# A delta rule's set-up in another order: the products for the inverse first, the other chunk products beside the substitution, their masks on GpSimd

## The chip, the core and the metric

The kernel runs on one core of a Trainium2 chip. The metric is the device time of one execution in microseconds (us), as the median of several runs of the same program. A core has five engines that run their own instruction streams and wait for one another by semaphores: TensorE (PE in the profile; its weight loads are PEld), VectorE (DVE), ScalarE (ACT), GpSimd (POOL) and SyncE (SP), which starts DMA transfers. Matrix products go to PSUM, a memory of eight banks, from which VectorE and ScalarE read them; everything else lies in SBUF, with 128 partitions.

## The reference

Two layers of a decoder trunk on one sequence of 512 tokens with 1024 channels, all in float32. Each layer has a feed-forward block, three token mixers on the same normalised input (an RWKV-7 delta rule, latent attention, an HGRN2 recurrence), whose outputs are gated and merged, and a second feed-forward block. The change is in the first mixer. It has 8 heads of 64 channels, and its state is updated token by token:

```python
def rwkv7_scan(r, w, k, v, kk, a):
    ...
    def step(state, inp):
        r_t, w_t, k_t, v_t, kk_t, a_t = inp
        sa = jnp.einsum('bhvk,bhk->bhv', state, -kk_t)
        state = (state * w_t[:, :, None, :]
                 + sa[..., None] * (kk_t * a_t)[:, :, None, :]
                 + v_t[..., None] * k_t[:, :, None, :])
        return state, jnp.einsum('bhvk,bhk->bhv', state, r_t)
```

## The kernel before

**Chunks instead of tokens.** The kernel cuts the 512 tokens into 8 chunks of 64 and handles a chunk at a time. Within a chunk it needs triangular matrices of products between tokens: for each head and chunk the left factors are two kinds of key (beta, which is `kk*a`, and the key `k`, together the tensor `BK`), and the right factors two kinds of query (alpha, the removal key, and rho, the receptance; together `AR`). Of these four products per chunk and head, beta·alpha gives a unit triangular matrix that has to be inverted; key·alpha multiplies the values later; and the two with rho go into the output. Each product is masked to its triangle.

**`rwkv_invert`** (from L463) makes these products, masks them and inverts. For each of four pairs of heads, 16 matmuls (L481) compute all four kinds at once: 128 weight columns by 128 moving columns, from 64 rows. They go into two PSUM banks at a time (the names `b` in the trace; three banks, 2 to 4, take turns under the use "a"). VectorE multiplies each full bank of 128x512 by the triangular mask on its way to SBUF (L484, 16 per layer). ScalarE then cuts the 32x32 diagonal blocks of beta·alpha out into one tile (L487, 16 copies per layer), VectorE transposes that tile (L489), and 31 steps of a forward substitution follow on VectorE, each a multiplication (L500) and a subtraction (L501). In step j the multiplication reads column j of the blocks, `a[:, j + 1:, j]`, whose elements lie 32 elements apart; `ti` is the inverse as it grows. GpSimd fills `ti` with zeros and a diagonal of ones beforehand (L492, L493). Two transposes (L504, L505) bring the result into the two forms that the next step needs. That next step (L522 and L525, small matmuls of 32x32) puts the 64x64 inverse together from its 32x32 blocks, and its first matmul needs the second transpose.

**`rwkv_scan`** follows: key·alpha times the values (L565) and then a loop over the eight chunks (L581 to L615).

**What else runs there.** TensorE has other work that doesn't depend on this chain: 41 column blocks of projections for the other two mixers and for the gates, in three matmuls per 128x128 weight (L251, L252, L253; 24 per block), called fillers here. Each weight is split first, into a rounded part on ScalarE (L208) and a rest on VectorE (L209). `pump` pulls blocks of them into the program at places named by a table, and a scheduler then sets a fixed order for each engine from the program's order, the data's dependencies and the buffers. In both layers fillers stand between the products and L522. In layer 0 the rotary key of the attention mixer runs there as well (VectorE L901 to L904 and L930, ScalarE L906, one matmul L932, ScalarE's copy L934), and it uses the same three PSUM banks.

Of the kernel before, what the change touches and what calls it, by code (L numbers as in the profile page):

```python
# [15 lines left out]
ALU = mybir.AluOpType  # L16
# [4 lines left out]
P = 128  # L21
# [3 lines left out]
NT = T // P  # L25
# [4 lines left out]
CH = 64  # L30
NC = T // CH
# [275 lines left out]
class Rwkv:  # L307
# [155 lines left out]
    def rwkv_invert(self):  # L463


        nc = self.nc
        S = self.S
        GM = S["GM"] = [self.slot(i, (P, 2, NC, P)) for i in (0, 1, 6, 7)]
        ad = self.m4((P, 4, 2, NT, 32))
        mask = self.c("tri").unsqueeze(1).broadcast_to([P, 4, P])  # L470
        for p in range(4):
            self.pump("A4", p)

            for i in range(2):
                ps = [self.psum("a", (P, 4, P)) for _ in range(2)]
                for c in range(4):
                    cc = 4 * i + c
                    for e in range(2):
                        q = slice(64 * e, 64 * e + 64)
                        bk = S["BK"][p // 2][q, p % 2].rearrange("p t z x -> p (t z x)")  # L480
                        nc.tensor.matmul(ps[e][:, c, :], bk[:, P * cc:P * cc + P], S["AR"][p // 2][q, p % 2, :, cc * CH:(cc + 1) * CH],  # L481
                                         start=True, stop=True)
                for e in range(2):
                    nc.vector.tensor_mul(GM[p][:, e, 4 * i:4 * i + 4, :], ps[e], mask)  # L484
            for b in range(4):
                q = slice(32 * b, 32 * b + 32)
                nc.scalar.copy(ad[q, p], GM[p][q, :, b // 2::2, 32 * (b % 2):32 * (b % 2) + 32])  # L487
        ac = [self.m4((P, 32, 32)) for _ in range(2)]
        nc.vector.transpose(out=ac[0], in_=ad.rearrange("p a e t x -> p x (a e t)"))  # L489
        a, tmp = ac  # L490
        ti = self.m4((P, 32, 32))
        nc.gpsimd.memset(ti, 0.0)  # L492
        nc.gpsimd.memset(ti.rearrange("p s t -> p (s t)")[:, ::33], 1.0)  # L493
        for j in range(31):
            if j % 4 == 0:
                self.pump("A9", j // 4)
            n, m = j + 1, 31 - j
            acol = a[:, j + 1:, j].unsqueeze(1).broadcast_to([P, n, m])
            trow = ti[:, :n, j].unsqueeze(2).broadcast_to([P, n, m])
            nc.vector.tensor_mul(tmp[:, :n, :m], acol, trow)  # L500
            nc.vector.tensor_sub(ti[:, :n, j + 1:], ti[:, :n, j + 1:], tmp[:, :n, :m])  # L501

        td, tu = self.m4((P, 32, 32)), self.m4((P, 32, 32))
        nc.vector.transpose(out=td.rearrange("p n t -> p t n"), in_=ti.rearrange("p s t -> p t s"))  # L504
        nc.vector.transpose(out=tu.rearrange("p n s -> p s n"), in_=ti)  # L505
        S["tt"] = [self.slot(2, (P, 16, P)), self.slot(3, (P, 16, P))]
        for i in range(2):
            tt = S["tt"][i]
            nc.gpsimd.memset(tt, 0.0)
            for b in range(4):  # L510
                q = slice(32 * b, 32 * b + 32)
                nc.scalar.copy(tt[q, :, q], td[q, 16 * i:16 * i + 16, :])

            self.pump("A5", i)
            n21, x = self.psum("a", (P, 16, 32)), self.t2(shape=(P, 16, 32))
            for half in range(2):
                for n in range(16):
                    h, t = 4 * i + n // 4, n % 4
                    for u in range(2):
                        up, dn = slice(64 * u, 64 * u + 32), slice(64 * u + 32, 64 * u + 64)  # L520
                        if half == 0:
                            nc.tensor.matmul(n21[dn, n, :], GM[h // 2][up, h % 2, 2 * t + u, 32:64], tu[up, 16 * i + n, :],  # L522
                                             start=True, stop=True, tile_position=(64 * u, 64 * u + 32))
                        else:
                            nc.tensor.matmul(n21[up, n, :], x[dn, n, :], tt[dn, n, dn], start=True, stop=True,  # L525
                                             tile_position=(64 * u + 32, 64 * u))
                for u in range(2):
                    up, dn = slice(64 * u, 64 * u + 32), slice(64 * u + 32, 64 * u + 64)
                    if half == 0:
                        nc.scalar.copy(x[dn], n21[dn])  # L530
                    else:
                        nc.scalar.activation(tt[up, :, dn], n21[up], AF.Copy, scale=-1.0)

        for p in range(4):
            self.pump("A6", p)
            bk = S["BK"][p // 2][:, p % 2].rearrange("p t z x -> p (t z x)")
            tmp = [self.t2() for _ in range(2)]
            for i in range(2):
                dl = self.DL[:, p, 4 * i:4 * i + 4].unsqueeze(2).broadcast_to([P, 4, P])
                nc.vector.tensor_mul(tmp[i].rearrange("p (c x) -> p c x", x=P), bk[:, 512 * i:512 * i + 512].rearrange("p (c x) -> p c x", x=P), dl)  # L540
            for i in range(2):
                ps = self.psum("a", (P, 4, P))
                for c in range(4):
                    self.transpose(ps[:, c, :], tmp[i][:, c * P:(c + 1) * P])
                nc.scalar.copy(bk[:, 512 * i:512 * i + 512].rearrange("p (c x) -> p c x", x=P), ps)

    def rwkv_scan(self, l):


        nc = self.nc  # L550
        S = self.S
        GM, vn = S["GM"], S["vn"]
        U = [slice(0, 64), slice(64, 128)]
        al = lambda p: S["AR"][p // 2][:, p % 2, 0]
        rho = lambda p: S["AR"][p // 2][:, p % 2, 1]
        bk = lambda p, c: S["BK"][p // 2][:, p % 2].rearrange("p t (u z) x -> p (t u) (z x)", u=2)[:, c]
        gv = [self.m4((P, 2, 2, NT, CH)) for _ in range(2)]
        for p in range(4):
            self.pump("A7", p)
            ps = self.psum("a", (P, 2, NT, CH))  # L560
            for e in range(2):
                h = 2 * p + e
                for t in range(NT):
                    for u in range(2):
                        nc.tensor.matmul(ps[U[u], e, t, :], GM[p][U[1 - u], e, 2 * t + u, 0:64], vn[U[1 - u], t, 64 * h:64 * h + 64], start=True, stop=True)  # L565
            nc.scalar.copy(gv[p // 2][:, p % 2], ps)
        for c in range(NC):
            self.pump("A8", c)
            t, u = c // 2, c % 2
            ck = slice(c * CH, (c + 1) * CH)  # L570

            zv = self.t2(shape=(P, 4, 2, CH))
# [3 lines left out]
            else:  # L576
                r = self.t2(shape=(P, 4, 2, CH))
                ps = [self.psum("a", (P, 4, CH)) for _ in range(2)]
# [7 lines left out]
            z = self.psum("z", (P, 4, 2, CH))  # L586
            for p in range(4):
                for e in range(2):
                    h = 2 * p + e
                    nc.tensor.matmul(z[U[u], p, e, :], S["tt"][h // 4][U[u], (h % 4) * 4 + t, U[u]], rhs(p, e), start=True, stop=True)  # L590
            nc.scalar.activation(zv[U[u]], z[U[u]], AF.Copy, scale=-1.0)
            y = self.psum("y", (P, 4, CH))
# [13 lines left out]

            for p in range(4):
                for e in range(2):
                    nc.tensor.matmul(y[U[e], p, :], zv[:, p, e, :], GM[p][:, e, c, 64:], start=p == 0, stop=c == 0 and p == 3)
            if c:  # L610
                for p in range(4):
                    for e in range(2):
# [796 lines left out]
```

## Time and profile before

| | us |
|---|---|
| median of 3 runs | 2726.13 |
| lowest and highest | 2724.97, 2731.2 |
| the profiled execution | 2736.01 |
| its span in the trace | 2734.2 |
| TensorE busy | 2683.8 (98%) |
| VectorE busy | 1779.8 (65%) |
| ScalarE busy | 1347.4 (49%) |
| GpSimd busy | 58.5 (2%) |

The mean clock that TensorE was granted over this execution was 0.989 of full speed. In rows of the timeline the columns are start, duration, engine, line, operation, output and inputs (partitions x elements), and in brackets the idle time before it and what ended that. A float32 matmul has two records in the trace. "Fillers" are L251 to L253 there.

### The profile page before, as it was taken

The numbers are of one execution on the slowest core, as the hardware profiler recorded it, in microseconds if no ns is written. First come the engines' busy times: TensorE is split into PE (matmuls) and PEld (weight loads), VectorE is DVE, ScalarE is ACT, GpSimd is POOL, SyncE is SP. The second block draws the span as 40 slices with busy tenths as digits, with TensorE's granted clock in tenths as the row PEclk, the third lists the DMA queues.
The fourth block names the chain that finished last, engine by engine and source line by source line (L and its number), as shares of the span: only waits on it lengthen the run. The fifth ranks groups of instructions, "written<-read, shape, count | busy, mean of one in ns | idle before, by whom it ended". The sixth has DMA issues, their size and how long they took to land. (4 is left out here: it accounts for less than half of the span.)

```text
span 2734.2 us, 42594 instructions
## 1 busy us (share of the span) xinstructions
PE 2683.8 (98%) x17669; PEld 2331.5 (85%) x17669; DVE 1779.8 (65%) x2507; ACT 1347.4 (49%) x2133; POOL 58.5 (2%) x121
## 2 busy tenths in 40 slices
PE   8999999989999999999999999999899999999999
PEld 7999887777787789998889998877677878899987
DVE  6786447763866667875467864477558676678843
ACT  4444346245657644444334443464465685444532
POOL 0000010000000000000000000100000000100000
PEclk9999999899999999999999999999999999999999
DMA  4333332324422451233313233323253225423332
GB/s 142 108 109 123 124 117 91 102 74 155 158 82 67 158 189 62 96 127 116 126 40 116 93 125 126 112 90 108 82 194 111 94 69 180 146 87 99 107 118 77
DMA packets 223518, 307.72 MB, mean 113 GB/s; under 512 B 11856, under 2 KB 181052, under 8 KB 221788
## 3 DMA queue, kind: packets, MB, share of 16 engines
q1 hardware_dynamic: 223324, 304.99, 33.2%
q8 instruction: 139, 2.28, 0.3%
q14 instruction: 55, 0.45, 0.0%
HBM read 269.84 MB, written 35.13 MB: 112 GB/s over the span
## 5 line engine op out<-in xcount | busy, mean ns | idle before, releaser
L253 PE MATMUL b<-xhi,wl 128*128 128x256 f32 (+1 forms) x2176 | 734.9, 338 | 0.0
L251 PE MATMUL b<-xhi,wh 128*128 128x256 f32 (+1 forms) x2176 | 734.9, 338 | 0.0
L252 PE MATMUL b<-xlo,wh 128*128 128x256 f32 (+1 forms) x2176 | 734.2, 337 | 0.0
L208 ACT CAST wh<-ws 128x1024 fp32r<-128x1024 f32 (+5 forms) x448 | 393.1, 889 | 649.7 <-PE b L252 273.5
L209 DVE TENSOR_TENSOR wl<-ws,wh 128x1024 fp32r<-128x1024 f32 (+5 forms) x448 | 453.1, 1022 | 258.9 <-ACT wh L208 255.6
L251 PEld LDWEIGHTS b<-xhi,wh 128*128 128x128 f32 x2176 | 415.3, 191 | 45.4 <-issue 4.4
L252 PEld LDWEIGHTS b<-xlo,wh 128*128 128x128 f32 x2176 | 415.3, 191 | 41.5 <-issue 3.2
L253 PEld LDWEIGHTS b<-xhi,wl 128*128 128x128 f32 x2176 | 415.2, 191 | 41.2 <-issue 1.9
L251 PE MATMUL b<-s,wh 128*128 128x256 f32 (+1 forms) x1120 | 344.4, 307 | 1.3 <-DVE s L996 1.3
L252 PE MATMUL b<-s,wh 128*128 128x256 f32 (+1 forms) x1120 | 344.1, 307 | 0.0
L253 PE MATMUL b<-s,wl 128*128 128x256 f32 (+1 forms) x1120 | 344.1, 307 | 0.0
L208 ACT CAST wh<-m 128x1024 fp32r<-128x1024 f32 x144 | 151.2, 1050 | 231.0 <-PE b L252 100.8
L251 PE MATMUL b<-wh,t 128*128 128x512 f32 x576 | 224.2, 389 | 0.0
L252 PE MATMUL b<-wl,t 128*128 128x512 f32 x576 | 224.1, 389 | 0.0
L253 PE MATMUL b<-wh,t 128*128 128x512 f32 x576 | 224.1, 389 | 0.0
L251 PEld LDWEIGHTS b<-s,wh 128*128 128x128 f32 x1120 | 213.9, 191 | 11.9 <-DVE s L996 2.2
L253 PEld LDWEIGHTS b<-s,wl 128*128 128x128 f32 x1120 | 213.9, 191 | 10.1
L252 PEld LDWEIGHTS b<-s,wh 128*128 128x128 f32 x1120 | 213.9, 191 | 9.8
L209 DVE TENSOR_TENSOR wl<-m,wh 128x1024 fp32r<-128x1024 f32 x144 | 174.0, 1224 | 33.3 <-ACT wh L208 33.3
L209 DVE TENSOR_TENSOR t<-s,t 128x512 fp32r<-128x512 f32 x80 | 55.0, 691 | 158.6 <-PE b L252 154.2
L251 PEld LDWEIGHTS b<-wh,t 128*128 128x128 f32 x576 | 108.1, 188 | 23.1 <-ACT t L1194 0.6
L253 PEld LDWEIGHTS b<-wh,t 128*128 128x128 f32 x576 | 108.1, 188 | 22.4
(328 smaller groups left out, 4002.2 us busy)
## 6 DMA issues: line engine op xcount, KB each, us to landing
ws<-in_w_in_dram SPq DMA_DIRECT2D x58, 1024.0 KB
ws<-in_ffn_w_up_dram SPq DMA_DIRECT2D x44, 1024.0 KB
ws<-in_ffn_w_down_dram SPq DMA_DIRECT2D x44, 1024.0 KB
ws<-in_ffn_w_gate_dram SPq DMA_DIRECT2D x43, 1024.0 KB
gd<-f SPq DMA_DIRECT2D x48, 256.0 KB
t<-gd SPq DMA_DIRECT2D x48, 256.0 KB
s<-cd SPq DMA_DIRECT2D x8, 1024.0 KB
ws<-in_w_o_dram SPq DMA_DIRECT2D x8, 1024.0 KB
```

Source lines behind the costliest of these rows:

```text
L208: self.nc.scalar.copy(hi, src)
L209: self.nc.vector.tensor_sub(lo, src, hi.bitcast(F32))
L251: nc.tensor.matmul(out, whi, xhi, start=start, stop=False, **kw)
L252: nc.tensor.matmul(out, whi, xlo, start=False, stop=False, **kw)
L253: nc.tensor.matmul(out, wlo, xhi, start=False, stop=stop, **kw)
```

## The change

Products and masks are split by kind, and reordered:

- Each product is now of one kind: 64 weight columns by 64 moving columns (L479 of the changed kernel, function `product`), 256 per layer, four times as many as of L481, each a quarter of its size. Results for even and odd chunks go to different halves of a bank.
- The 64 beta·alpha products come first. VectorE masks them (L495, 4 per layer), ScalarE cuts out the diagonal blocks (L498, 16 copies as before), and VectorE transposes (L500).
- That transpose writes its output in another arrangement, so the substitution reads its column contiguously: `a[:, j, j + 1:]` (L528; the subtraction is L529).
- The other 192 products come behind this in the program. ScalarE copies each full bank to SBUF (L508, 12 per layer), and GpSimd multiplies it by the mask in place (L509, 12 per layer, 128x512, both operands in SBUF).
- The readers of the products index the new tiles. `pump("A4", ...)` has zeros in its table before and after.

The transposes behind the substitution are L532 and L533 now, the combining matmuls L550 and L553, the memsets on GpSimd L503, L504 and L537, the rotary key's steps L930 to L933, L959, L935, L961 and L963.

```diff
-        GM = S["GM"] = [self.slot(i, (P, 2, NC, P)) for i in (0, 1, 6, 7)]
+        GA, GR = S["GA"], S["GR"] = [[self.slot(i) for i in x] for x in ((0, 1), (6, 7))]
...
+        def product(out, p, e, c, z, i):
+            bk = S["BK"][p // 2][U[e], p % 2].rearrange("p t z x -> p (t z) x")
+            nc.tensor.matmul(out[U[z]], bk[:, 2 * c + z, :], S["AR"][p // 2][U[e], p % 2, i, c * CH:(c + 1) * CH], start=True, stop=True)
+        def alphas(i, y):
+            ps = [self.psum("a", (P, 2, NT, CH)) for _ in range(2)]
+            for k in range(2):
+                for c in range(NC):
                     for e in range(2):
-                        nc.tensor.matmul(ps[e][:, c, :], bk[:, P * cc:P * cc + P], S["AR"][p // 2][q, p % 2, :, cc * CH:(cc + 1) * CH],
-                                         start=True, stop=True)
-                for e in range(2):
-                    nc.vector.tensor_mul(GM[p][:, e, 4 * i:4 * i + 4, :], ps[e], mask)
-            for b in range(4):
-                nc.scalar.copy(ad[q, p], GM[p][q, :, b // 2::2, 32 * (b % 2):32 * (b % 2) + 32])
+                        product(ps[e][:, k, c // 2, :], 2 * i + k, e, c, (c + y) % 2, 0)
+            return [x.rearrange("p k t x -> p (k t) x") for x in ps]
+        for i in range(2):
+            ps = alphas(i, 0)
+            for e in range(2):
+                nc.vector.tensor_mul(by8(GA[i][:, e]), ps[e], mask[0])
+                for b in range(4):
+                    q = slice(32 * b, 32 * b + 32)
+                    nc.scalar.copy(ad[q, 2 * i:2 * i + 2, e], GA[i][:, e].rearrange("p (k t x) -> p k t x", k=2, x=CH)[q, :, :, 32 * (b % 2):32 * (b % 2) + 32])
-        nc.vector.transpose(out=ac[0], in_=ad.rearrange("p a e t x -> p x (a e t)"))
+        nc.vector.transpose(out=ac[0].rearrange("p s t -> p t s"), in_=ad.rearrange("p a e t x -> p x (a e t)"))
...
+        def finish(out, ps, mk):
+            nc.scalar.copy(by8(out), ps)
+            nc.gpsimd.tensor_tensor(by8(out), by8(out), mk, op=ALU.mult)
+        for i in range(2):
+            for e, ps in enumerate(alphas(i, 1)):
+                finish(GA[i][:, 2 + e], ps, mask[0])
+        for p in range(4):
+            ps = [self.psum("a", (P, NC, CH)) for _ in range(2)]
+            for c in range(NC):
+                for z in range(2):
+                    for e in range(2):
+                        product(ps[e][:, c, :], p, e, c, z, 1)
+            for e in range(2):
+                finish(GR[p // 2][:, 2 * (p % 2) + e], ps[e], mask[1])
         for j in range(31):
...
-            acol = a[:, j + 1:, j].unsqueeze(1).broadcast_to([P, n, m])
+            acol = a[:, j, j + 1:].unsqueeze(1).broadcast_to([P, n, m])
```

**On VectorE, in layer 1, at the end of the products** (`s` are the masked products in SBUF, `b` PSUM banks, `m` the tiles of the substitution). Before:

```order
L484 TENSOR_TENSOR s_2467_17043<-b_2482_17130,consts_64 128x512
L484 TENSOR_TENSOR s_2467_17043<-b_2483_17141,consts_64 128x512
L484 TENSOR_TENSOR s_2467_17043<-b_2484_17142,consts_64 128x512
L209 TENSOR_TENSOR wl_17337<-ws_17302,wh_17336 128x1024
L489 STREAM_TRANSPOSE m_17157<-m_17044 128x1024
L500 TENSOR_TENSOR m_17158<-m_17157,m_17160 128x31
L501 TENSOR_TENSOR m_17160<-m_17160,m_17158 128x31
```

After:

```order
L457 SCALAR_TENSOR_TENSOR s_2409_16984<-mean_17232,b_2459_17227 128x4x128
L495 TENSOR_TENSOR s_2464_17244<-b_2469_17249,consts_64 128x512
L495 TENSOR_TENSOR s_2464_17244<-b_2470_17250,consts_64 128x512
L495 TENSOR_TENSOR s_2465_17245<-b_2471_17293,consts_64 128x512
L495 TENSOR_TENSOR s_2465_17245<-b_2472_17294,consts_64 128x512
L500 STREAM_TRANSPOSE m_17337<-m_17248 128x32x32
L528 TENSOR_TENSOR m_17338<-m_17337,m_17340 128x31
L529 TENSOR_TENSOR m_17340<-m_17340,m_17338 128x31
```

Sixteen masks stood between L457 and the transpose before (the last three are shown), and four stand there now; one L209 has moved from there into later rows. Between the first L528 and L532 stand three L209 in layer 1 and four in layer 0, where six stood in both layers.

**On GpSimd, in layer 1** (`m_17340` is `ti`, the tile that the substitution fills; `m_17160` before). Before:

```order
L509 MEMSET s_2496_17264 128x2048
L509 MEMSET s_2495_17263 128x2048
L492 MEMSET m_17160 128x1024
L493 MEMSET m_17160 128x32
```

After:

```order
L537 MEMSET s_2496_17672 128x2048
L537 MEMSET s_2495_17671 128x2048
L503 MEMSET m_17340 128x1024
L509 TENSOR_TENSOR s_2464_17244<-s_2464_17244,consts_64 128x512
L504 MEMSET m_17340 128x32
L509 TENSOR_TENSOR s_2464_17244<-s_2464_17244,consts_64 128x512
L509 TENSOR_TENSOR s_2465_17245<-s_2465_17245,consts_64 128x512 x2
L509 TENSOR_TENSOR s_2466_17246<-s_2466_17246,consts_64 128x512 x4
L509 TENSOR_TENSOR s_2467_17247<-s_2467_17247,consts_64 128x512 x4
```

One mask stands ahead of the diagonal of ones (L504), for which the first L528 waits; the other eleven stand behind it. In layer 0 six stand ahead of it and six behind.

**On VectorE, in layer 0, around the fourth mask** (`t_4714` and `rope_4670` belong to the rotary key, `s_652` to its tables). Before:

```order
L901 TENSOR_SCALAR s_652_4627<-s_652_4627 128x512
L484 TENSOR_TENSOR s_666_4721<-b_676_4765,consts_64 128x512
L903 SCALAR_TENSOR_TENSOR s_652_4627<-s_652_4627 32x512 x2
L904 TENSOR_SCALAR s_652_4627<-s_652_4627 32x512 x2
L484 TENSOR_TENSOR s_666_4721<-b_677_4766,consts_64 128x512
L484 TENSOR_TENSOR s_667_4722<-b_679_4782,consts_64 128x512
L484 TENSOR_TENSOR s_667_4722<-b_680_4793,consts_64 128x512
L930 TENSOR_TENSOR t_4714<-b_661_4689,rope_4670 64x512
L484 TENSOR_TENSOR s_668_4723<-b_682_4809,consts_64 128x512
L484 TENSOR_TENSOR s_668_4723<-b_683_4810,consts_64 128x512
L484 TENSOR_TENSOR s_665_4720<-b_672_4737,consts_64 128x512
```

After:

```order
L495 TENSOR_TENSOR s_666_4721<-b_673_4770,consts_64 128x512
L900 SCALAR_TENSOR_TENSOR s_652_4627<-s_652_4627 128x512
L930 TENSOR_SCALAR s_652_4627<-s_652_4627 128x512
L932 SCALAR_TENSOR_TENSOR s_652_4627<-s_652_4627 32x512 x2
L933 TENSOR_SCALAR s_652_4627<-s_652_4627 32x512 x2
L959 TENSOR_TENSOR t_4714<-b_661_4689,rope_4670 64x512
L495 TENSOR_TENSOR s_666_4721<-b_672_4769,consts_64 128x512
L500 STREAM_TRANSPOSE m_4813<-m_4724 128x32x32
```

The rotary key's steps, which stood among sixteen masks before, now stand ahead of the fourth and last mask, whose bank (`b_672`) is the one that the rotary key's product holds until ScalarE has copied it (L963). ScalarE has there 12 copies L498, two L508, the table load and the rope L935, two L508, the key's copy L963, one L508, the last four L498 and then the other seven L508.

**On TensorE** the fillers between the first product and the first L522 (L550 now) are 190 before and 123 after in layer 0, 163 and 93 in layer 1; behind the last product they are 149 and 101, and 150 and 78. No filler stands ahead of the first product that didn't before, and none is dropped: 67 and 70 stand behind L550 now.

More of the change, by code (lines that the diff above doesn't have):

```diff
@@ L467, in rwkv_invert @@
         S = self.S
-        GM = S["GM"] = [self.slot(i, (P, 2, NC, P)) for i in (0, 1, 6, 7)]
+        GA, GR = S["GA"], S["GR"] = [[self.slot(i) for i in x] for x in ((0, 1), (6, 7))]
+        U = [slice(0, 64), slice(64, 128)]
+        by8 = lambda x: x.rearrange("p (c x) -> p c x", x=CH)
+        alpha = S["alpha"] = lambda z, h: GA[h // 4][:, 2 * z + h % 2].rearrange("p (k t x) -> p k t x", k=2, x=CH)[:, h // 2 % 2]
         ad = self.m4((P, 4, 2, NT, 32))
-        mask = self.c("tri").unsqueeze(1).broadcast_to([P, 4, P])
@@ L471, in rwkv_invert @@
[L471 to L477, printed above, removed]
-                    for e in range(2):
-                        q = slice(64 * e, 64 * e + 64)
-                        bk = S["BK"][p // 2][q, p % 2].rearrange("p t z x -> p (t z x)")
-                        nc.tensor.matmul(ps[e][:, c, :], bk[:, P * cc:P * cc + P], S["AR"][p // 2][q, p % 2, :, cc * CH:(cc + 1) * CH],
-                                         start=True, stop=True)
-                for e in range(2):
-                    nc.vector.tensor_mul(GM[p][:, e, 4 * i:4 * i + 4, :], ps[e], mask)
-            for b in range(4):
-                q = slice(32 * b, 32 * b + 32)
-                nc.scalar.copy(ad[q, p], GM[p][q, :, b // 2::2, 32 * (b % 2):32 * (b % 2) + 32])
+        mask = [self.c("tri")[:, o].unsqueeze(1).broadcast_to([P, NC, CH]) for o in U]
@@ L488, in rwkv_invert @@
+        for i in range(2):
+            self.pump("A4", i)
+            ps = alphas(i, 0)
[4 more added lines that the diff above has]
+                    nc.scalar.copy(ad[q, 2 * i:2 * i + 2, e], GA[i][:, e].rearrange("p (k t x) -> p k t x", k=2, x=CH)[q, :, :, 32 * (b % 2):32 * (b % 2) + 32])
         ac = [self.m4((P, 32, 32)) for _ in range(2)]
-        nc.vector.transpose(out=ac[0], in_=ad.rearrange("p a e t x -> p x (a e t)"))
+        nc.vector.transpose(out=ac[0].rearrange("p s t -> p t s"), in_=ad.rearrange("p a e t x -> p x (a e t)"))
@@ L521, in rwkv_invert @@
                         if half == 0:
-                            nc.tensor.matmul(n21[dn, n, :], GM[h // 2][up, h % 2, 2 * t + u, 32:64], tu[up, 16 * i + n, :],
+                            nc.tensor.matmul(n21[dn, n, :], alpha(0, h)[up, t, 32:64], tu[up, 16 * i + n, :],
                                              start=True, stop=True, tile_position=(64 * u, 64 * u + 32))
@@ L551, in rwkv_scan @@
         S = self.S
-        GM, vn = S["GM"], S["vn"]
+        vn = S["vn"]
+        gr = lambda p, e, c: S["GR"][p // 2][:, 2 * (p % 2) + e, c * CH:(c + 1) * CH]
         U = [slice(0, 64), slice(64, 128)]
@@ L564, in rwkv_scan @@
                     for u in range(2):
-                        nc.tensor.matmul(ps[U[u], e, t, :], GM[p][U[1 - u], e, 2 * t + u, 0:64], vn[U[1 - u], t, 64 * h:64 * h + 64], start=True, stop=True)
+                        nc.tensor.matmul(ps[U[u], e, t, :], S["alpha"](1, h)[U[1 - u], t, :], vn[U[1 - u], t, 64 * h:64 * h + 64], start=True, stop=True)
             nc.scalar.copy(gv[p // 2][:, p % 2], ps)
@@ L608, in rwkv_scan @@
                 for e in range(2):
-                    nc.tensor.matmul(y[U[e], p, :], zv[:, p, e, :], GM[p][:, e, c, 64:], start=p == 0, stop=c == 0 and p == 3)
+                    nc.tensor.matmul(y[U[e], p, :], zv[:, p, e, :], gr(p, e, c), start=p == 0, stop=c == 0 and p == 3)
             if c:
```

## The prediction

> **What bounds the kernel now.** I read the page's busy shares first, then the waits of TensorE, then the windows around the two longest of them, then the timelines of VectorE, ScalarE and GpSimd there. The profiled execution took 2736.01 us and its span is 2734.2 us; it lies 9.9 us above the median of the runs, 2726.13 us. I work out a difference against the profiled execution and put it on the median. About 0.2% (5.5 us) is what a measurement of this kernel can tell from no change.
>
> The page's busy line, then the head of the waits of TensorE (who waited for whom: total us, times, longest):
> ```profile
> PE 2683.8 (98%) x17669; PEld 2331.5 (85%) x17669; DVE 1779.8 (65%) x2507; ACT 1347.4 (49%) x2133; POOL 58.5 (2%) x121
> ```
> ```profile
> PE b L522 <- DVE m L505: 16.7, 2, 8.6
> PE b L204 <- DVE m L288: 9.1, 4, 8.2
> ```
> TensorE is busy 98% of the time, so the kernel is bound by TensorE and little can be won outside its 50 us of idle time (2734.2 − 2683.8). A third of that is one wait, once in each layer: the first L522 waits for the transposes behind the substitution. Windows of 10 us (PE, PEld, DVE, ACT, POOL busy; then PE clock, DMA share, GB/s):
> ```profile
> 580.00:590.00 10.00, 2.96 (x14) 2.11 (x12) 9.48 (x20) 0.61 (x1) 0.00 (x0) 0.86 0.26 78
> 590.00:600.00 10.00, 8.87 (x200) 7.61 (x201) 4.08 (x6) 7.20 (x13) 0.00 (x0) 0.50 0.08 29
> 620.00:630.00 10.00, 10.00 (x154) 7.49 (x154) 2.44 (x8) 2.85 (x6) 0.00 (x0) 1.00 0.01 2
> 1930.00:1940.00 10.00, 1.43 (x23) 0.96 (x23) 9.55 (x19) 2.25 (x4) 0.00 (x0) 0.77 0.48 154
> 1940.00:1950.00 10.00, 10.00 (x196) 8.46 (x191) 2.39 (x4) 7.10 (x13) 0.00 (x0) 0.55 0.01 3
> ```
> VectorE is full (9.5 of 10) while TensorE stands; after the wait TensorE runs its next 10 us at clocks of 0.50 and 0.55 (about 5 us and 4.5 us more lost). In the scan behind it TensorE is full again at 1.00, so a filler matmul that is pushed back there costs its whole time. The rule of my sum follows: per layer, change = (new start of the first L550 − old start of the first L522) + (time of the fillers that no longer stand before it). What TensorE does earlier than that start changes nothing as long as it still has to wait there.
>
> The chain to that start, in both layers (start us, us, instruction):
> ```profile
> 553.63 0.21 DVE L500 TENSOR_TENSOR m<-m,m 128x31 f32<-128x31 f32 x1
> 591.13 2.08 PE L522 MATMUL b<-m,s 32*32 32x32 f32 x70 [8.17 <-DVE m L505]
> ```
> ```profile
> 1902.94 0.21 DVE L500 TENSOR_TENSOR m<-m,m 128x31 f32<-128x31 f32 x1
> 1939.53 1.67 PE L522 MATMUL b<-m,s 32*32 32x32 f32 x55 [8.57 <-DVE m L505]
> ```
> From the first L500 to L522 it is 37.5 us in layer 0 and 36.6 us in layer 1.
>
> **The moved fillers.** By the order of TensorE 67 filler matmuls fewer stand before L550 in layer 0 and 70 fewer in layer 1. Filler to filler, 24 steps apart:
> ```profile
> 1925.14 0.39 PE L253 MATMUL b<-xhi,wl 128*128 128x512 f32 x1
> 1930.58 0.39 PE L253 MATMUL b<-xhi,wl 128*128 128x512 f32 x1
> ```
> 5.44 / 24 = 0.227 us each: 15.2 us and 15.9 us that come later. This is the price that the earlier start has to beat.
>
> **The earlier start, layer 1.** Only four masks instead of sixteen now stand on VectorE, behind the L457 that ends at 1884.1.
> ```profile
> 1883.46 0.68 DVE L457 SCALAR_TENSOR_TENSOR s<-mean,b 128x512 f32<-128x512 f32 x1
> 1885.45 1.98 DVE L484 TENSOR_TENSOR s<-b,consts 128x512 f32<-128x512 f32 x3 [0.71 <-PE b L481]
> 1900.74 2.09 DVE L489 STREAM_TRANSPOSE m<-m 128x1024 f32<-128x1024 f32 x1 [0.32 <-ACT m L487]
> ```
> ```profile
> 1890.92 1.65 ACT L487 COPY m<-s 32x256 f32<-32x256 f32 x4 [1.82 <-DVE s L484]
> 1899.07 1.64 ACT L487 COPY m<-s 32x256 f32<-32x256 f32 x4
> ```
> The first mask ends at 1884.8; from there ScalarE has 16 copies of the same size, 4 x 1.65 = 6.6 us, to 1891.4 (it is later than the masks, 4 x 0.66). The transpose takes 2.1 us: the substitution starts at about 1893.6, not 1902.9. Its ones-diagonal (L504) stands on GpSimd behind one mask, which follows the first copy L508: 1891.4 + 0.6 + about 1.1 + 0.15 = 1893.2, just in time. The products are no bound: 64x64x64 matmuls run at
> ```profile
> 607.81 2.08 PE L565 MATMUL b<-s,s 64*64 64x64 f32 x64
> ```
> (64 records, 32 matmuls) 0.065 us each, so 64 of them are 4.2 us, beside the copies.
>
> **Layer 0.** Here the fourth mask waits for a PSUM bank that the rotary key holds. Before, that key came late, because its steps stood behind masks that waited for products:
> ```profile
> 515.92 0.69 DVE L484 TENSOR_TENSOR s<-b,consts 128x512 f32<-128x512 f32 x1
> 521.09 0.86 DVE L904 TENSOR_SCALAR s<-s 32x512 f32<-32x512 f32 x2
> 530.53 0.69 DVE L930 TENSOR_TENSOR t<-b,rope 64x512 f32<-64x512 f32 x1
> ```
> ```profile
> 532.00 1.91 PE L932 MATMUL b<-t,consts 64*128 64x512 f32 x2
> ```
> ```profile
> 510.83 1.28 ACT L906 ACT_TABLE_LOAD   x1
> 521.99 0.72 ACT L906 ACTIVATE rope<-s,consts 128x512 f32<-128x512 f32 x1 [9.88 <-DVE s L904]
> 533.95 0.58 ACT L934 COPY kr<-b 128x512 f32<-128x512 f32 x1 [11.24 <-PE b L932]
> ```
> Now ScalarE has 12 copies (third mask's end 515.4 + 1.65 to 518.0), two L508 (1.2), the table load (1.28) and the rope (0.72): 521.1. Then L959 0.7, its matmul 1.9, the key's copy 0.6: 524.4. Then 16 products at 0.065 to 0.13 (to 525.9), the mask 0.7, four copies 1.65, the transpose 2.1 and 0.1: the substitution starts at about 530.5, not 553.6. GpSimd has its second memset behind the rope (to 522.9), then the masks as the copies bring them, and L504 at about 530.
>
> **The substitution itself.** The groups of the window 1900 to 1940 on VectorE (busy us, mean ns), and the 256-element step (16x16) by form:
> ```profile
> L500 DVE TENSOR_TENSOR m<-m,m 128x31 f32<-128x31 f32 (+15 forms) x31 | 14.8, 478 | 1.0
> L501 DVE TENSOR_TENSOR m<-m,m 128x31 f32<-128x31 f32 (+15 forms) x31 | 10.6, 343 | 1.0
> L209 DVE TENSOR_TENSOR wl<-ws,wh 128x1024 fp32r<-128x1024 f32 x6 | 7.3, 1220 | 1.4 <-ACT wh L208 1.4
> ```
> L500 and L501 have the same sizes; L500 alone reads a column with a stride of 32. If the stride is the whole difference, the contiguous column saves 14.8 − 10.6 = 4.2 us a layer; the other bound is 0. I take 4.2, since L501 also reads two operands, one of them in pieces of row length, and no other difference but a repeated value is left. Of the six L209 (1.22 us each) four stay inside in layer 0 and three in layer 1: −2.4 and −3.7 us. So the chain is 37.5 − 4.2 − 2.4 = 30.9 us and 36.6 − 4.2 − 3.7 = 28.7 us, and L550 could start at 561.4 and 1922.3. TensorE is there earlier in layer 0: products to about 533, 101 fillers, 556. In layer 1 the products wait in pairs of banks for the copies L508 and end between 1899 and 1906; with 78 fillers TensorE is there at 1917 to 1924, about when VectorE is. Without anything else: layer 0 561.4 − 591.1 + 15.2 = −14.5 us, layer 1 1922.3 − 1939.5 + 15.9 = −1.3 us, together −15.8 us.
>
> **The masks on GpSimd.** 12 per layer, 128x512, reading two tensors in SBUF. The trace has no such instruction, but it shows what small ones do beside VectorE (GpSimd first, VectorE second):
> ```profile
> 427.35 0.19 POOL L417 COPY DL<-s 128x8 f32<-128x8 f32 x1 [0.94 <-ACT s L406]
> 430.53 0.53 POOL L417 COPY DL<-s 128x8 f32<-128x8 f32 x1 [2.99 <-ACT s L406]
> 1800.44 0.55 POOL L417 COPY DL<-s 128x8 f32<-128x8 f32 x1 [2.99 <-ACT s L406]
> ```
> ```profile
> 429.79 1.22 DVE L209 TENSOR_TENSOR wl<-ws,wh 128x1024 fp32r<-128x1024 f32 x1
> 1799.73 1.22 DVE L209 TENSOR_TENSOR wl<-ws,wh 128x1024 fp32r<-128x1024 f32 x1
> ```
> The same copy of 8 elements takes 0.19 us when VectorE stands, and 0.53 and 0.55 us when it falls into an L209, which reads two SBUF tensors: it ends at 431.06 and 1800.99, 0.05 us behind the L209s' ends at 431.01 and 1800.95. It was held until VectorE was done. The Trainium skill, "SBUF — State Buffer", section "Who interferes with whom", says just that: a VectorE instruction with two SBUF inputs and a GpSimd one that reads SBUF exclude each other, and the second to issue blocks for the whole of the first. The rows agree for GpSimd as the one held; that VectorE is held by GpSimd no row here shows. If one port serves both engines, the one that comes second waits, whichever it is; so I take it to hold both ways. All 62 instructions of a substitution read two SBUF tensors, and each waits for the one before, so a mask gets in at the next boundary and VectorE then stands for the mask's length. By the order and the times above six masks fall into the substitution in layer 0 and eleven in layer 1. The length of one, by the memset of the same engine:
> ```profile
> 524.51 0.95 POOL L492 MEMSET m<- 128x1024 f32 x1
> ```
> 512 written elements are 0.48 us at that rate, the lower bound; two reads and a write one after the other 1.43 us, the upper. I take 1.05, above the middle because two inputs must come in. The Trainium skill, "GPSIMD Engine Reference", section "3.1 Elementwise — side-by-side cycle accounting", measures 4497 ns for 2048 elements of a two-input add; a quarter is an estimate of 1.12 us, and the sum would be +3.2 us by it. No run here shows that figure yet. With 1.05: 17 x 1.05 = 17.9 us, all on the chain, since VectorE is late in both layers. L550 starts at 567.7 and 1933.9.
>
> **Sum.** −15.8 + 17.9 = +2.1 us: 2738.1 us against the profiled execution, 2728 us on the median, no measurable change. Layer 0 gives about −8 and layer 1 takes +10. With the bounds of the mask's length it is −7.7 (0.48) to +8.5 (1.43). The half clock behind the wait stays in both layers, since a wait of 10 us and more stays.
>
> **Rivals.**
> - *The masks cost VectorE nothing* (the lock holds GpSimd only, or the masks slip between). For it: VectorE's rows beside the small copies are no longer than elsewhere (1.22). Then −15.8 us, 2710 us; and if TensorE arrives last in layer 1, the half clock there goes too (4.5 us): 2706 us.
> - *Slower: the contiguous column saves nothing*, while the masks block. For it: L528 still reads one value repeated along the row, which L501 doesn't. Then 2 x 4.2 = 8.4 us come back: +10.5 us, 2737 us. With masks of 1.05 us the change is slower by over 5.5 us once the column saves less than 2.5 us a layer.
> - *Neither*: masks free, column no gain. −15.8 + 8.4 = −7.4 us, 2719 us: only the earlier start is left.
>
> **Chances.** The forecast 0.45, masks free 0.25, slower 0.20, neither 0.10. Faster by over 0.2%: all of the masks-free case, two thirds of the last and a fifth of the forecast (short masks), 0.40. Slower: nearly all of its rival and a sixth of the forecast (long masks), 0.25. The rest 0.35. The range reaches from the masks-free case to the slower rival with masks somewhat longer than mine, 2707 to 2740 us; the forecast's own range is 2718 to 2735 us.
>
> **What would show it.** In the changed profile: L509 on GpSimd near 1.05 us when alone; L528 and L529 with a few instances about 1 us longer than the rest, six and eleven of them; the 16x16 L528 near 0.43 us instead of 0.63; the wait of L550 for L533 about 10 us in layer 0 and 10 to 17 us in layer 1; the first L528 near 530.5 and 1893.6. I would be wrong if the substitution shows no long instances, if TensorE arrives at L550 last, or if fillers behind it find idle time.

## The result

The changed kernel is slower: 2746.05 us (median of 4 runs, 2743.11 to 2747.3) against 2728.66 us for the kernel before on the same chip, a ratio of 1.0063 with a 95% interval of 1.0046 to 1.008. The forecast was 2728 us with a range of 2707 to 2740 us. A second series gave 2739.41 against 2725.55 us, 1.0059 (1.0046 to 1.0071). Not every execution of one kernel has TensorE's full clock in layer 0, and the experiments below show that this matters here.

The profiled execution took 2746.48 us, its span is 2744.4 us. The busy line of its page and the head of TensorE's waits:

```profile
PE 2684.4 (98%) x18437; PEld 2332.9 (85%) x18437; DVE 1773.3 (65%) x2483; ACT 1364.1 (50%) x2159; POOL 89.1 (3%) x145
```
```profile
PE b L550 <- DVE m L533: 15.7, 2, 9.0
PE b L204 <- DVE m L288: 9.1, 4, 8.1
PE b L253 <- DVE wl L209: 6.3, 1, 6.3
```

TensorE still waits 15.7 us for the end of the substitution (16.7 before), 6.7 us in layer 0 and 9.0 us in layer 1. A third row is new: in layer 1 a filler waits 6.3 us for its weight's rest, which VectorE computes between two steps of the same substitution.

In layer 1, VectorE's substitution and GpSimd's masks (start us, us):

```profile
1893.02 1.03 DVE L528 TENSOR_TENSOR m<-m,m 128x31 f32<-128x31 f32 x1
1894.09 1.20 DVE L529 TENSOR_TENSOR m<-m,m 128x31 f32<-128x31 f32 x1
1895.32 1.22 DVE L528 TENSOR_TENSOR m<-m,m 128x60 f32<-128x60 f32 x1
...
1905.51 1.30 DVE L528 TENSOR_TENSOR m<-m,m 128x156 f32<-128x156 f32 x1
1906.85 0.32 DVE L529 TENSOR_TENSOR m<-m,m 128x156 f32<-128x156 f32 x1
...
1914.88 0.42 DVE L528 TENSOR_TENSOR m<-m,m 128x256 f32<-128x256 f32 x1
```
```profile
1892.65 0.17 POOL L504 MEMSET m<- 128x32 f32 x1
1892.73 13.90 POOL L509 TENSOR_TENSOR s<-s,consts 128x512 f32<-128x512 f32 x11
```

While the eleven masks run, from 1892.7 to 1906.6, each step of VectorE takes 1.0 to 1.3 us, whatever its size: one mask, one step, in turn. The eleven masks take 13.90 us, 1.26 us each, no longer than one takes alone (1.27 us): GpSimd loses nothing, VectorE bears the whole cost. The first step, of 31 elements, takes 1.03 us here and took 0.21 us before. As soon as the masks end, a step of 156 elements takes 0.32 us. The 16x16 step takes 0.42 us. With the strided column, in the kernel before, it took 0.63 us:

```profile
1918.30 0.63 DVE L500 TENSOR_TENSOR m<-m,m 128x256 f32<-128x256 f32 x1
```

The groups of both windows (535 to 575, then 1892 to 1935):

```profile
L528 DVE TENSOR_TENSOR m<-m,m 128x31 f32<-128x31 f32 (+15 forms) x31 | 13.7, 440 | 1.1
L529 DVE TENSOR_TENSOR m<-m,m 128x31 f32<-128x31 f32 (+15 forms) x31 | 13.6, 439 | 1.0
```
```profile
L528 DVE TENSOR_TENSOR m<-m,m 128x31 f32<-128x31 f32 (+15 forms) x31 | 16.4, 529 | 1.1
L529 DVE TENSOR_TENSOR m<-m,m 128x31 f32<-128x31 f32 (+15 forms) x31 | 15.5, 500 | 1.0
```

They are 27.3 and 31.9 us. Without masks, below, they are 21.2 us in each layer. So the masks cost 6.1 us in layer 0 and 10.7 us in layer 1.

The start of the substitution in layer 0, on VectorE, with the rotary key's matmul on TensorE:

```profile
521.13 0.69 DVE L959 TENSOR_TENSOR t<-b,rope 64x512 f32<-64x512 f32 x1 [2.42 <-ACT rope L935]
532.33 0.69 DVE L495 TENSOR_TENSOR s<-b,consts 128x512 f32<-128x512 f32 x1 [10.50 <-PE b L479]
...
537.29 0.19 DVE L528 TENSOR_TENSOR m<-m,m 128x31 f32<-128x31 f32 x1
```
```profile
527.23 2.07 PE L961 MATMUL b<-t,consts 64*128 64x512 f32 x2
...
574.69 3.62 PE L550 MATMUL b<-m,s 32*32 32x32 f32 x128 [6.68 <-DVE m L533]
```

L959 came on time (forecast 521.1). But TensorE reached the key's matmul only at 527.2, and the substitution started at 537.3 instead of 530.5. TensorE's clock was at a half there (windows of 10 us, the clock is the third number from the end):

```profile
520.00:530.00 10.00, 10.00 (x90) 7.13 (x91) 0.69 (x1) 2.85 (x5) 5.43 (x4) 0.50 0.00 0
530.00:540.00 10.00, 9.95 (x204) 9.76 (x202) 5.29 (x9) 3.26 (x7) 4.82 (x5) 0.50 0.01 4
```

Two runs below without masks differ in the same way: at full clock the key's matmul starts at 523.0 and the substitution at 530.7, at half clock at 526.6 and 536.6. So it is the clock that puts off the start, and not the masks.

In layer 1 the substitution started at 1893.0 (forecast 1893.6) and L550 at 1934.0 (forecast 1933.9). That these times agree is partly luck: the forecast counted them from L457's end in the first trace, 1884.1, without the 8 us that layer 0 was to win. L457 now ends at 1883.5, so layer 0 as a whole won 0.7 us instead of 8; from L457's end to the end of the span it is 10.9 us longer than before, where the forecast for layer 1 was +10.

### The profile page after: what moved, and what is told of

Read it like the earlier page. It is cut to its first block, busy times and chain, and to the rows that moved or that the text cites. A ratio compares the mean times of both kernels' runs of the same rounds, so it can differ in the third digit from the quotient of the medians.

```text
span 2744.4 us, 44165 instructions
## 1 busy us (share of the span) xinstructions
PE 2684.4 (98%) x18437; PEld 2332.9 (85%) x18437; DVE 1773.3 (65%) x2483; ACT 1364.1 (50%) x2159; POOL 89.1 (3%) x145
## 5 line engine op out<-in xcount | busy, mean ns | idle before, releaser
L209 DVE TENSOR_TENSOR wl<-ws,wh 128x1024 fp32r<-128x1024 f32 (+5 forms) x448 | 453.2, 1022 | 285.1 <-ACT wh L208 279.6
L209 DVE TENSOR_TENSOR wl<-m,wh 128x1024 fp32r<-128x1024 f32 x144 | 173.9, 1223 | 33.8 <-ACT wh L208 33.8
L209 DVE TENSOR_TENSOR t<-s,t 128x512 fp32r<-128x512 f32 x80 | 54.9, 690 | 158.4 <-PE b L252 154.2
```

Of the source, the lines that this page charges most:

```text
L209: self.nc.vector.tensor_sub(lo, src, hi.bitcast(F32))
```

## The experiments

### The kernel before, once more

The same program, unchanged.

> The kernel before, unchanged, once more with a profile, to see what the first profile of it (2736.01 us, 7 us above the median of its runs) had in excess. Theory 1 (the excess is in this kernel's product stage: TensorE's half clock of layer 0 from 515 to 543 us is there in some executions only): a profile near 2728 us, with less time at 0.50 there. Theory 2 (the excess lies elsewhere, or the profile itself costs it): the same 28 us at 0.50 in layer 0, and the time near 2736 again or the 7 us missing in another stage. Timed: 2728, ratio 1.000.

Measured: 2725.22 us, a ratio of 1.0002 (0.9988 to 1.0016), with its profile at 2724.61 us. The windows of the new profile, and its two L522:

```profile
510.00:520.00 10.00, 9.45 (x53) 7.11 (x54) 8.99 (x17) 1.97 (x2) 1.81 (x1) 1.00 0.49 175
520.00:530.00 10.00, 10.00 (x65) 8.04 (x64) 6.23 (x10) 2.99 (x5) 2.85 (x3) 1.00 0.00 0
530.00:540.00 10.00, 10.00 (x52) 7.65 (x51) 3.52 (x6) 6.53 (x17) 0.00 (x0) 1.00 0.44 133
```
```profile
579.50 3.62 PE L522 MATMUL b<-m,s 32*32 32x32 f32 x128 [8.17 <-DVE m L505]
...
1927.08 3.62 PE L522 MATMUL b<-m,s 32*32 32x32 f32 x128 [8.53 <-DVE m L505]
```

The clock is 1.00 here, where the first profile of this kernel has these rows:

```profile
520.00:530.00 10.00, 10.00 (x35) 7.98 (x34) 3.44 (x7) 0.72 (x1) 2.85 (x3) 0.50 0.00 0
530.00:540.00 10.00, 10.00 (x44) 7.93 (x43) 5.10 (x7) 3.08 (x6) 0.00 (x0) 0.50 0.00 0
```

L522 of layer 0 starts at 579.5 in the new profile and started at 591.1 in the first profile. From L522 of one layer to that of the next it is 1347.6 us here and 1348.4 us in the first profile: the difference lies ahead of L522 in layer 0, where the two profiles differ by this half clock. Theory 1 stands. Of the 29 executions of the kernel before in this series 23 lie between 2723.5 and 2726.5 us, with a mean clock of 0.993 or 0.994, five between 2736.1 and 2739.2 us at 0.988 or 0.989, and one between. My prediction was worked out from one of the few: the profile's 2736.01 us.

### The changed kernel, once more

The same program, unchanged.

> The changed kernel, unchanged, in more executions and with a second profile. The kernel before has a half clock in layer 0's product stage in about one execution in six (2736 to 2739 us, else 2723 to 2726). Theory 1 (the same luck here): two groups, one near 2738 to 2740 us without that half clock, in which the masks alone make the loss, and one near 2746. Theory 2 (the changed kernel brings the half clock about, since TensorE waits there for a mask and a copy): nearly all executions at 2743 to 2747 us, and a profile with 0.50 from 515 to 545 us.

Measured: 2738.54, 2738.71, 2739.41 us at a mean clock of 0.993, 2743.57 at 0.989, and the profiled one, 2746.57 at 0.987. Theory 1 again: there are two groups, though the changed kernel falls into the upper one more often (six of nine executions in both series, if 2743 and above are counted) than the kernel before. Within this series the medians of the lower groups are 2738.7 and 2725.5 us, so without the half clock the change costs 13 us; at the top there are one execution of 2746.6 us and two of the kernel before at 2736.6 us, 10 us apart. That the changed kernel's lower group is the one without the half clock rests on its mean clock, 0.993: both profiles of it (2746.48 and 2746.57 us) have the half clock.

### No masks

```diff
-            nc.scalar.copy(by8(out), ps)
-            nc.gpsimd.tensor_tensor(by8(out), by8(out), mk, op=ALU.mult)
+            nc.scalar.activation(by8(out), ps, AF.Copy, scale=0.0)
```

> The changed kernel without the 12 masks per layer on GpSimd (ScalarE's copies write zeros instead of the products, so the output is not the reference's). Theory A (the port's lock: each mask that falls into the substitution holds VectorE for about 1.0 us, 6 in layer 0 and 11 in layer 1): L528 and L529 have no instance over 0.45 us, L550 starts 6 us earlier in layer 0 and, limited by TensorE's own arrival, 9 us earlier in layer 1: 15 us less than the changed kernel, about 2731 us, up to 20 less if the half clock behind the wait of layer 1 goes too. Theory B (the lock does not cost; the loss is the moved fillers and the later start of layer 0): no more than 3 us less, 2743 us or above.

Measured: 2724.41 us, 0.9997 of the kernel before (0.9983 to 1.0011), and 15 to 22 us below the changed kernel's two medians. The lines behind the edit move up by one: L527 and L528 are the two kinds of step here, L549 is the combining matmul. The steps by line (ns, min/median/max), and the two starts behind the substitution:

```profile
L527 DVE TENSOR_TENSOR m<-m,m x62: 191/359/426, 530.7 to 1905.0; 128x31 f32<-128x31 f32 x4, 128x60 f32<-128x60 f32 x4, 128x87 f32<-128x87 f32 x4, 128x112 f32<-128x112 f32 x4
L528 DVE TENSOR_TENSOR m<-m,m x62: 191/358/425, 530.9 to 1905.3; 128x31 f32<-128x31 f32 x4, 128x60 f32<-128x60 f32 x4, 128x87 f32<-128x87 f32 x4, 128x112 f32<-128x112 f32 x4
```
```profile
562.05 3.62 PE L549 MATMUL b<-m,s 32*32 32x32 f32 x128 [4.43 <-DVE m L532]
...
1909.41 3.62 PE L549 MATMUL b<-m,s 32*32 32x32 f32 x128 [5.20 <-DVE m L532]
```

No step is over 0.43 us, and the first matmul starts at 562.05, where the prediction had 561.4 without masks. Theory A stands. And without the masks the rest of the change gives next to nothing: the matmul starts 17.4 us earlier than in the repeated profile of before (579.50), and 67 fillers (15.2 us) stand behind it now; in layer 1, counted from L457's end, it starts 15.5 us earlier, with 70 fillers (15.9 us) behind it. The profiled executions of the two, both without the half clock in layer 0's products, are 1.8 us apart (2722.85 and 2724.61).

### Memsets in place of the masks

```diff
-            nc.scalar.copy(by8(out), ps)
-            nc.gpsimd.tensor_tensor(by8(out), by8(out), mk, op=ALU.mult)
+            nc.scalar.activation(by8(out), ps, AF.Copy, scale=0.0)
+            for _ in range(2):
+                nc.gpsimd.memset(out, 0.0)
```

> The changed kernel without its masks (ScalarE's copies write zeros, the output is not the reference's), and in place of each mask two memsets of the same 128x512 tile on GpSimd, 2 x 0.48 us, which write SBUF and read nothing. Theory A (what holds VectorE is the shared read port): VectorE's instructions as short as without masks, 2722 to 2726 us. Rival (any work of GpSimd on SBUF holds VectorE): 6 and 11 holds of about 0.8 us, 2736 to 2740 us.

Measured: 2728.33 us, 1.0006 (0.9996 to 1.0015). The median is 4 us above that of the run without masks and 2 us above theory A's range, and far below the rival's. Why it is above is not shown; the profiled execution has the half clock in layer 0 and again from 1887 to 1897. What tells the theories apart is the length of the steps. GpSimd and VectorE in layer 1 (L529 and L530 are the steps here, from 1886.6 on):

```profile
1885.52 7.08 POOL L510 MEMSET s<- 128x512 f32 x15
1893.30 1.95 POOL L510 MEMSET s<- 128x512 f32 x4 [0.70 <-ACT s L508]
```
```profile
L529 DVE TENSOR_TENSOR m<-m,m 128x31 f32<-128x31 f32 (+15 forms) x31 | 10.6, 343 | 1.1
L530 DVE TENSOR_TENSOR m<-m,m 128x31 f32<-128x31 f32 (+15 forms) x31 | 10.6, 343 | 1.0
```

GpSimd is busy beside the substitution and only writes; VectorE's two groups are 21.2 us, as without masks. So GpSimd's writing does not hold VectorE. What a mask does beyond a memset is to read two tensors and multiply them. That the reading counts, and not the multiplying, is likely, since the small copies in the prediction's rows, which read and don't multiply, were held by VectorE; no run separates the two here. The Trainium skill, "SBUF — State Buffer", section "Who interferes with whom", says that a GpSimd instruction which only writes does not contend with such steps. These rows agree.

### Masks on VectorE

```diff
-            nc.scalar.copy(by8(out), ps)
-            nc.gpsimd.tensor_tensor(by8(out), by8(out), mk, op=ALU.mult)
+            nc.vector.tensor_mul(by8(out), ps, mk)
```

> The changed kernel with the 12 masks per layer on VectorE, straight from PSUM (one multiplication of 0.66 us in place of ScalarE's copy and GpSimd's). By the order four stand inside the substitution of layer 0 and ten inside that of layer 1. Theory A (a mask on GpSimd costs VectorE about 1.0 us, more than doing it): against the 2724 us without masks 4 x 0.66 + 10 x 0.66 = 9 us more, about 2733 us, some 13 less than the changed kernel. Rival (offloading is worth its while, VectorE is the late engine): 2746 us or more.

Measured: 2730.35 us, 1.0019 (1.0005 to 1.0033), half of its ten executions between 2723.5 and 2726.3 us and half between 2734.4 and 2739.7. Against the changed kernel it is 9 to 16 us less. The scheduler set another order for it: 26 and 32 more fillers stand ahead of L549 than in the changed kernel, so the two don't differ by the masks alone. That a mask on VectorE is cheaper for VectorE than on GpSimd is shown by the durations, about 0.65 us for one against 1.0 us of holding (L508 is the mask here):

```profile
1887.57 1.29 DVE L508 TENSOR_TENSOR s<-b,consts 128x512 f32<-128x512 f32 x2 [0.50 <-PE b L479]
```

Theory A is supported; the size of its gain is not separated from the order.

### Masks behind the substitution

```diff
+        tri = self.t2(shape=(P, 2 * CH))
+        nc.vector.scalar_tensor_tensor(tri, tu.rearrange("p n s -> p (n s)")[:, :2 * CH], 0.0, self.c("tri"), op0=ALU.mult, op1=ALU.add)
+        for out, o in late:
+            nc.gpsimd.tensor_tensor(by8(out), by8(out), tri[:, o].unsqueeze(1).broadcast_to([P, NC, CH]), op=ALU.mult)
```

> The changed kernel with the same 12 masks per layer on GpSimd, made to wait for the substitution (their mask tile is written by VectorE behind L533, at 0.25 us). Theory A (lock): the substitution runs as without masks; the masks, 12 x 1.27 = 15 us, end before the scan needs them (30 us later in layer 0), and hold up L568 and a few L209 instead, which nobody waits for soon: 12 to 18 us less than the changed kernel, 2728 to 2734 us. Theory B: no gain, 2746 us, or more where the scan waits for a mask.

Measured: 2730.08 us, 1.0008 (0.9992 to 1.0023), its executions 2725.85 to 2737.22. Theory A stands: the substitution runs unheld (no step over 0.43 us), and L556, the combining matmul here, starts at 562.04 as without masks, though all twelve masks are made. The masks are L539 here, and VectorE's next work is L574 (L568 in the changed kernel), multiplications that also read two tensors in SBUF. The two in layer 0:

```profile
562.30 16.55 POOL L539 TENSOR_TENSOR s<-s,t 128x512 f32<-128x512 f32 x12 [37.92 <-DVE t L537]
```
```profile
562.14 4.03 DVE L574 TENSOR_TENSOR t<-s,DL 128x512 f32<-128x512 f32 x3
569.21 1.09 DVE L574 TENSOR_TENSOR t<-s,DL 128x512 f32<-128x512 f32 x1 [3.04 <-PE b L559]
578.88 2.50 DVE L574 TENSOR_TENSOR t<-s,DL 128x512 f32<-128x512 f32 x4 [8.58 <-POOL s L539]
```

Three L574 take 4.03 us beside the masks, and four take 2.50 us when the masks are done. The wait of 8.58 us is of my making: the mask's tile (L537) comes from the pool that L574 writes to.

### Masks late, and more fillers ahead

```diff
-        tri = self.t2(shape=(P, 2 * CH))
+        tri = tmp.rearrange("p s t -> p (s t)")[:, :2 * CH]
...
-    "A7": (2, 0, 1, 0), "A8": (0, 0, 0, 0, 1, 0, 1, 0), "A9": (0, 0, 0, 0, 0, 0, 1, 0), "C": 11,
+    "A7": (2, 0, 1, 0), "A8": (0, 0, 0, 0, 1, 0, 1, 0), "A9": (0, 0, 1, 0, 0, 0, 1, 0), "C": 11,
```

> The masks on GpSimd behind the substitution, their mask tile now in a tile that is free by then (so that L574 does not wait for GpSimd), and one more filler block asked for beside the substitution; by the order 22 more fillers stand ahead of L556 in layer 1, none more in layer 0. Theory (TensorE's wait of 6.4 us in layer 1 is only filled by moving work ahead of it): 22 x 0.227 = 5.0 us less than with the masks late alone, and the half clock behind that wait (about 4.5 us) gone if under 3 us of it are left: 2717 to 2723 us, below both kernels. Rival (the wait is VectorE's and grows by as much): 2726 to 2730 us.

Measured: 2727.81 us, 1.0005 (0.9995 to 1.0015), its executions 2723.16 to 2732.45. TensorE's wait for L535 fell to 4.1 us in both layers together (10.9 with the masks late alone). In layer 0, where no filler was added, it is 2.4 us; there the products ran in part at half clock (0.50 from 520 to 525), and TensorE came later. In layer 1 it fell from 6.4 to 1.7 us, as the 22 fillers (5.0 us) were to make it. But the profile shows half the clock behind it again, 0.62 from 570 to 580 and 0.53 from 1920 to 1930, and TensorE has new waits there:

```profile
1914.86 3.05 PE L556 MATMUL b<-m,s 32*32 32x32 f32 x127 [1.70 <-DVE m L535]
...
1922.49 3.86 PE L559 MATMUL b<-s,t 32*32 32x32 f32 x128 [1.25 <-ACT t L564]
```

From L556 in layer 1 to the end of the span it is 1.7 us less than with the masks late alone, not 5.0. The median is 2.3 us lower, which the two intervals can't tell from nothing, and it isn't below the kernel before. The forecast of 2717 to 2723 failed: a wait of 1.7 us did not spare the half clock, and most of the fillers' time did not come back.

### The strided column in the changed kernel

```diff
-        nc.vector.transpose(out=ac[0].rearrange("p s t -> p t s"), in_=ad.rearrange("p a e t x -> p x (a e t)"))
+        nc.vector.transpose(out=ac[0], in_=ad.rearrange("p a e t x -> p x (a e t)"))
...
-            acol = a[:, j, j + 1:].unsqueeze(1).broadcast_to([P, n, m])
+            acol = a[:, j + 1:, j].unsqueeze(1).broadcast_to([P, n, m])
```

> The changed kernel with the column of the substitution read with a stride of 32 again and the transpose written as before. If the stride alone made L500 slower than L501: the 16x16 step takes 0.63 us instead of 0.42, the substitution is 4.2 us longer in each layer, less what hides behind masks, and L550 starts as much later: 6 to 8 us more than the changed kernel, 2753 us. Rival (the stride costs nothing by itself): 2746 us, with L528 at 0.42.

Measured: 2751.87 us, 1.0094 (1.0075 to 1.0112), and a profile at 2753.15 us, 6.7 us above that of the changed kernel, both with the half clock in layer 0:

```profile
577.83 3.62 PE L550 MATMUL b<-m,s 32*32 32x32 f32 x128 [9.93 <-DVE m L533]
...
1940.56 3.62 PE L550 MATMUL b<-m,s 32*32 32x32 f32 x128 [9.59 <-DVE m L533]
```

L550 starts 3.1 us later in layer 0 and 6.5 us later in layer 1, both layers' loss. The 16x16 step takes 0.59 us here (forecast 0.63, contiguous 0.42). So the column pays about 3.3 us a layer here, the rest of its 4.2 being hidden in steps that a mask holds anyway.

### The contiguous column alone

The kernel before, with the two lines of the last diff the other way round and nothing else.

> The kernel before with one part of the change alone: the transpose writes its output in the other arrangement and the substitution reads its column contiguously. Products, masks and fillers stand as before. Theory (the column is the part that pays, the reordering pays for itself with the fillers that it pushes back): L500 falls to L501's length, the substitution is 4.2 us shorter in each layer, and as TensorE waits 8.2 and 8.5 us for it, all of that comes off: 8.4 us less than the kernel before, 2717 us. If the half clock behind a wait of 4 us goes too, up to 9 us more. Rival (the new arrangement makes the transpose or the steps slower): no gain, 2725 us.

Measured: 2717.15 us against 2725.41 us, 0.9972 (0.9957 to 0.9986). Groups in layer 0 and the two starts:

```profile
L500 DVE TENSOR_TENSOR m<-m,m 128x31 f32<-128x31 f32 (+15 forms) x31 | 10.6, 343 | 1.0
L501 DVE TENSOR_TENSOR m<-m,m 128x31 f32<-128x31 f32 (+15 forms) x31 | 10.6, 342 | 1.0
```
```profile
575.25 3.62 PE L522 MATMUL b<-m,s 32*32 32x32 f32 x128 [4.08 <-DVE m L505]
...
1919.41 3.62 PE L522 MATMUL b<-m,s 32*32 32x32 f32 x128 [4.51 <-DVE m L505]
```

The mean of L500 falls from 478 to 343 ns, the length of L501, and the wait of TensorE from 8.2 and 8.5 us to 4.1 and 4.5 us. This is the fastest version of this study, 8.3 us below the kernel before and 22 to 29 us below the changed kernel's two medians.

## Why the prediction was wrong

- **The base of the sum: the step that failed.** The prediction worked out a difference against the profiled execution and put it on the median, 9.9 us lower. It noted the 9.9 us and did not ask where they lay. They lay in the stage that the change shortens: the half clock at 515 to 543 us in layer 0 had put L522 at 591.1, and in the repeated profile, which stands for 23 of 29 executions by its time and mean clock, it starts at 579.5. The new start, 561.4, was worked out from products and fillers at full clock (0.065 and 0.227 us each). So layer 0 took an old start at half clock from a new one at full clock, and counted the difference as a gain of the change. With 579.5 and all other terms as they stood, layer 0 without masks is 561.4 − 579.5 + 15.2 = −2.9 us, not −14.5, and the sum −4.2 + 17.9 = +13.7 us instead of +2.1. Measured between the lower groups: +13. A sign of it was in the first trace: the same products ran at 0.50 in layer 0 and at 1.00 in layer 1.
- **The start of the substitution in layer 0** (530.5) was right for an execution at full clock: the first step stands at 530.7 without masks. In the changed kernel's profiles, at half clock, it was 537.3 and 537.0, because TensorE reached the rotary key's matmul 5.4 us late. That is why the difference of the two first profiles, +10.5 us, came out above +2.1 as well.
- **The lock** held both ways, as taken: 16.8 us in six and eleven steps, forecast 17.9. That the size came out is luck: two errors cancel. A mask takes 1.27 us alone instead of 1.05, and by the rule that VectorE stands for the mask's whole length 17 of them would be 21.6 us. But a mask and a step in turn take 1.26 us together, hardly more than the mask alone, so each costs VectorE that less the step's own length, about 1.0 us. The rival of free masks is refuted by the runs without masks and with memsets.
- **The column** gained what its row said, 4.2 us a layer (10.6 for 14.8). The rival that it gains nothing, my only slower one, is refuted. The change was slower by another way.
- **The waits of L550** came out at 6.7 and 9.0 us, forecast about 10 and 10 to 17. In layer 0 TensorE came late for its half clock; in layer 1 it had been held for 6.3 us before, by the filler that waits for L209.
- **The price of the moved fillers** stood: without the masks the change is level with the kernel before (0.9997), a start 17.4 us earlier against 15.2 us of fillers in layer 0. Behind the first combining matmul it is 15.5 us longer to the next layer's first product, and 15.9 us longer in layer 1 to the end of the span, than in the repeated profile of before; forecast 15.2 and 15.9.
- **The chances.** I gave 0.25 to slower, for a column that fails or masks longer than 1.05 us. A rival on the base itself (the profiled execution being one of few) was missing, and it would have carried the sum over the bound.

What stays open: what brings the half clock about. It comes in some executions of one and the same program, with TensorE busy 10 of 10 us; the Trainium skill, "TensorE: Matmul & The Clock Gate", section "Part 1: The HAM clock gate", speaks of a free-running window and of transitions that differ from run to run, which agrees as far as chance goes, but it gives a busy engine its full clock back after about 3.4 us, and here it stayed away for 27 us. The traces say a little more. By their clock records every stretch at half clock, but for the one at the very end of each span, lasts 3.41 us or a whole multiple of it, up to nine (30.7 us). And in all eleven profiles TensorE waits 0.5 to 1.2 us at about 513 us, among the first products; in six of them a half clock begins 1.7 to 2.8 us later, in five none does. Many small matmuls follow in every case; whether it is these that keep the clock down, once it is down, is a rival that no run tests. Why the changed kernel has it more often wasn't tried either.

## What to carry to other kernels

Where a profiled execution lies above the median of its runs, find the stage that holds the excess before a difference is worked out against it; if the change touches that stage, the excess is part of the forecast gain and not there in other executions. Work that is moved to GpSimd to relieve VectorE is not free when both read two tensors from SBUF: here each mask of 1.27 us cost VectorE 1.0 us, more than the 0.65 us of doing it. An earlier start on a full engine is worth only the wait that is left, less the work that no longer stands ahead of it; of this change the two lines on the column were the gain, 8.3 us.

## What the runs showed that I had not expected

- VectorE and GpSimd took strict turns, one step to one mask, for 14 us in layer 1, and the loss was VectorE's; even a step of 31 elements (0.19 to 0.21 us alone) took 1.0 to 1.2 us.
- A mask of 128x512 with two operands in SBUF took 1.27 us on GpSimd with VectorE idle. A quarter of the 4497 ns that the Trainium skill, "GPSIMD Engine Reference", section "3.1 Elementwise — side-by-side cycle accounting", gives for 2048 elements is an estimate of 1.12 us: this row is 13% longer.
- A wait of TensorE of 4.1 to 4.5 us was followed by half a clock, as one of 8.5 us was: the windows 1920 to 1930 show 0.50 with the column alone, and 0.57 in the repeated profile of before. A wait of 1.7 us was followed by it as well (0.53, masks late with more fillers).
